# Attention of a hybrid layer on one core: a third k2 buffer in the second half, and another order on VectorE and ScalarE at the end

## The chip, the cores and the metric

The kernel is one program on one core of a Trainium2 chip. The core has a matrix engine (TensorE, PE in the profile; PEld is its loading of weights), a vector engine (VectorE, DVE), a scalar engine (ScalarE, ACT), a general engine (GpSimd, POOL) and a queue engine that mostly issues DMAs (SyncE, SP). Each engine runs its own list of instructions in order and waits on semaphores for the others. All share an on-chip memory, SBUF, of 128 partitions, and the matmuls write to PSUM.

The metric is the device time of one execution in microseconds (us); the median of several executions is given. A trace was taken of one more execution, the profiled one, and everything read from "the profile" or "the trace" belongs to it. L12 is line 12 of the kernel before.

## The reference

The layer has three groups of mixers that read one input projection (an LRU, an attention with forgetting gates, an RWKV-7 recurrence), an output projection, and a gated feed-forward network. The working length is 2064: 16 learned meta tokens, then 2048 tokens. The change lies in the attention (8 heads of 64) and in the start of the output projection:

```python
h += RMSNorm_post( W_out [ RG-LRU group | forgetting-attention group | RWKV-7 group ] ( W_in RMSNorm_pre(h) ) )
h += RMSNorm_post( W_down( gelu(g) * v ) ),  [g | v] = causal_dwconv3( W_up RMSNorm_pre(h) )
```

```python
c = jnp.cumsum(log_f, axis=1)
...
s = einsum('bhqd,bhkd->bhqk', qb, kh) + (cb[..., :, None] - c[..., None, :])
s = jnp.where(kpos[None, :] <= qpos[:, None], s, -jnp.inf)
p = jax.nn.softmax(s, axis=-1)
return einsum('bhqk,bhkd->bhqd', p, vh)
```

Here c is the running sum of the log forget gates of the head. The output must agree with this in float32, so the kernel splits many operands into a rounded high part and the rest (a "split": rounding on ScalarE, subtraction on VectorE) and multiplies the parts.

## The kernel before

**Stages.** The input projection runs first, with the recurrences of the LRU and RWKV groups interleaved. The attention follows; the recurrences' tail runs beside its first part. Then come the output projection in tiles of tokens, the feed-forward network's upper products, and its lower ones. The instructions are written as a Python program; a planner lays them out in lists for the engines. It may move work ahead of what the program says, by its estimate of when inputs are ready. Memory comes from pools. A pool marked `early` may be laid over the space of another that is not yet closed. `tc.issue_after(x)` is an order given by hand: what is made inside the block stands behind instruction x in the list of x's engine (only there).

**The attention.** It goes in two halves: blocks of 512 queries 0 and 1, then 2 and 3; in each half head after head, and for each head its two blocks. A step is one head and one block. For each step there is

- `keys` (once a head): loads three operands. k1 holds the high part and the rest of the keys (L526, L527). k2 holds the keys' high part in its upper 64 rows (L522), a row of ones, and below it two rows of the forget sums, ch and cl (L524, L525). v1 holds the values, whose loads are issued a little later. In the second half a head's keys take a whole buffer; in the first half, half a buffer.
- `maxima`: scores of queries with k2 for the row maximum (L561, with a mask matmul L563 on the diagonal piece), each piece reduced on VectorE (L566); at the end the maximum is turned into a row of the query operand q2 (L571, transposes L574, L575).
- `weights`: the scores (L688 with k1, L689 with k2), the exponential (L693, ACT), the products with the values (L711), and the sum of the weights over the keys in `acc` (L732; one addition in four on VectorE, the others on GpSimd). A group of four key tiles has its values' products one group later.
- `ending`, at the end of a step: the halves of the products are added (L745 on ACT, L748 on DVE). Then three parts are put off by 2, 7 and 12 ticks. `total` splits `acc` (rounding L755 on ACT, subtraction L756 on POOL), sums it over the partitions by two matmuls (L758, L759), copies the sum out (L760) and sends it through memory so that it lies across partitions (L761, L762). `invert` takes reciprocals (L766) and broadcasts them back by two DMAs (L767, L768). `scale` multiplies (L771) and stores the mixed outputs (L772).

`tick` (L797) takes the parts that are due and gives them the order behind `self.reduced`, the latest reduction of a maximum. `run` (L809) interleaves: the maxima are two steps ahead of the weights (`AHEAD = 2`). So after the last maxima two steps of weights are left with no maxima beside them, (7,2) and (7,3) as head and block; the last group of values and the `ending` of (6,3) are written inside (7,2). After them come the parts still put off, and on the last step the DMAs go through GpSimd's queue.

**The buffers.** `Attn.__init__` makes two sets (k1, k2, v1), and `next("k")` (L490) goes round among them; the fixed rows of k2 are written once (`fixed`, L487 and L488, on GpSimd). Since L689 reads k2, a k2 buffer is free again when the scores of its head's second step are done. SBUF pools grow from the left or from the right end. On the right lie `pad`, a tile that only takes up room, and next to it `mt` for the small attention of the meta tokens' own queries, which runs beside the second half (`meta`). Both, and the attention's pool on the left, overlap in space with pools of the input projection and the recurrences, which are closed by then or later. The recurrences' last operations are L1341 (DVE) and L1343 (a store).

**The output tiles.** `w_out_tile` takes 17 tiles of tokens. It loads a tile of the mixed outputs into the one buffer "wr" (L167), splits it into mh (L168, ACT) and ml (L169, DVE), and multiplies it with both parts of the weights: 2 halves of 24 matmuls (L174 to L176). Two tiles' mh and ml fit at once. Tiles 0 to 6 run inside the attention. Tiles 7 and 8 (`HELD = 7, 8`) are ordered behind the values of the last step but one (`at.steps[-2]`). From tile 8 on (`LATE, NORMS = 8, 2`) each tile is followed in the program by the feed-forward norm of up to two tiles: `ffn_norm` scales (L1599, into a buffer that lies over the attention's pool), transposes on PE (L1604) and copies out with `evac` (L57). `evac` goes to ACT and DVE in turn, and when it goes to ACT it stores the instruction in `core.acted`:

```python
self.flip ^= 1
if self.flip:
    self.acted = self.nc.scalar.activation(out, src, AF.Copy)
else:
    self.nc.vector.tensor_copy(out, src)
```

Of the kernel before, what the change touches and what calls it, by code (L numbers as in the profile page):

```python
# [8 lines left out]
F32 = mybir.dt.float32  # L9
F32R = mybir.dt.float32r  # L10
BF16 = mybir.dt.bfloat16
I32 = mybir.dt.int32  # L12
AF = mybir.ActivationFunctionType
ALU = mybir.AluOpType
# [4 lines left out]
P = 128  # L19
D = 1024  # L20
KD = D // P
META = 16
# [423 lines left out]
class Attn:  # L446
# [6 lines left out]

    def __init__(self, core, pool, psum, more, scr):
        self.core, self.pool, self.psum, self.more, self.scr = core, pool, psum, more, scr
        self.wide, self.bank, self.place = False, 0, 0
        nc = self.nc = core.nc
        self.clock, self.later, self.serial, self.added = 0, [], 0, 0
        self.pending, self.loads, self.steps, self.beside = None, [], [], iter(())


        self.turn = {"k": 1, "q2": 0, "q3": 0}
        self.ring = {s: [] for s in self.turn}
        for i in range(self.AHEAD + 1):
            q3 = pool.tile([P, 512], F32R, tag=f"q3_{i}", name=core.n("q3"), bufs=1)
            self.fixed(q3, None, self.ONES)
            self.ring["q3"].append(q3)
            q2 = pool.tile([P, 512], F32R, tag=f"q2_{i}", name=core.n("q2"), bufs=1)
            nc.vector.memset(q2[64:128].bitcast(F32), 0.0)
            self.ring["q2"].append(q2)  # L470
            if i > 1:
                continue
            k1 = pool.tile([P, 2, KHALF], F32R, tag=f"k1_{i}", name=core.n("k1"), bufs=1)
            k2 = pool.tile([P, 2, KHALF], F32R, tag=f"k2_{i}", name=core.n("k2"), bufs=1)
            v1 = pool.tile([P, 2, NKT // 2 + 1, 64], F32, tag=f"v1_{i}", name=core.n("v1"), bufs=1)
            self.fixed(None, k2, self.ONES)
            self.ring["k"].append((k1, k2, v1))

    def fixed(self, q, k, ones):

# [9 lines left out]
    def next(self, s):  # L490
        self.turn[s] = (self.turn[s] + 1) % len(self.ring[s])
        return self.ring[s][self.turn[s]]
# [14 lines left out]
    def keys(self, h, nt):  # L507

        nc, scr = self.nc, self.scr
        n = META + P * (nt - 1)  # L510
        r = slice(64 * h, 64 * h + 64)
        if n <= KHALF:

            i, half = divmod(self.place, 2)
            self.place = (self.place + 1) % 4
            k1, k2, v1 = (t[:, half] for t in self.ring["k"][i])
        else:
            k1, k2, v1 = self.next("k")
            k1, k2 = (t[:].rearrange("p h t -> p (h t)") for t in (k1, k2))
            v1 = v1[:].rearrange("p h j d -> p (h j) d")  # L520
        k1f, k2f = k1.bitcast(F32), k2.bitcast(F32)
        nc.sync.dma_start(k2f[0:64, :n], scr["kh"][r, :n])  # L522
        g = 64 + self.ONES
        nc.sync.dma_start(k2f[g : g + 1, :n], scr["ch"][h : h + 1, :n])  # L524
        nc.sync.dma_start(k2f[g + 1 : g + 2, :n], scr["cl"][h : h + 1, :n])  # L525
        nc.sync.dma_start(k1f[0:64, :n], scr["kh"][r, :n])  # L526
        nc.sync.dma_start(k1f[64:128, :n], scr["kl"][r, :n])  # L527

        def values():
            nc.sync.dma_start(v1[:, : nt - 1], scr["v"][: n - META, r].rearrange("(j p) d -> p j d", p=P))  # L530
            nc.sync.dma_start(v1[:META, nt - 1], scr["v"][n - META : n, r])


        self.loads.append(values)
        return k1, k2, v1
# [120 lines left out]
    def weights(self, h, b, keys, queries, fill):  # L656
# [80 lines left out]
        def ending(po, acc):  # L737


            while len(self.later) > 8:  # L740
                self.later.pop(0)[2]()

            o, oh = self.t([64, 512], "o", bufs=4), self.t([64, 512], "oh")
            c1 = kt[1][2]
            nc.scalar.activation(oh[:, c1:n], po[64:128, c1:n], AF.Copy)  # L745
            if c1:
                nc.scalar.activation(o[:, :c1], po[0:64, :c1], AF.Copy)
            nc.vector.tensor_tensor(o[:, c1:n], po[0:64, c1:n], oh[:, c1:n], op=ALU.add)  # L748
            g = n // 16
            dcol = self.t([16, 32], "dcol", bufs=4)  # L750
            rb, queue = [], self.queue

            def total():
                ah, al = (self.t([P, 512], "oh", F32R) for _ in range(2))
                nc.scalar.activation(ah[:, :n], acc[:, :n], AF.Copy)  # L755
                nc.gpsimd.tensor_tensor(al[:, :n], acc[:, :n], ah[:, :n], op=ALU.subtract)  # L756
                ps = self.mx()
                nc.tensor.matmul(ps[0:1, :n], core.ones_col[:], ah[:, :n], start=True, stop=False)  # L758
                nc.tensor.matmul(ps[0:1, :n], core.ones_col[:], al[:, :n], start=False, stop=True)  # L759
                nc.scalar.activation(acc[0:1, :n], ps[0:1, :n], AF.Copy)  # L760
                queue.dma_start(scr["den"][h : h + 1, ts], acc[0:1, :n])  # L761
                queue.dma_start(dcol[:, :g], scr["den"][h, ts].rearrange("(p c) -> p c", c=g))  # L762

            def invert():
                rb.append(self.t([64, 512], "rb"))
                nc.vector.reciprocal(dcol[:, :g], dcol[:, :g])  # L766
                queue.dma_start(scr["rden"][h, ts].rearrange("(p c) -> p c", c=g), dcol[:, :g])  # L767
                queue.dma_start(rb[0][:, :n], scr["rden"][h : h + 1, ts].broadcast_to([64, n]))  # L768

            def scale():  # L770
                nc.vector.tensor_tensor(o[:, :n], o[:, :n], rb[0][:, :n], op=ALU.mult)  # L771
                queue.dma_start(scr["mix"][256 + 64 * h : 256 + 64 * h + 64, ts], o[:, :n])  # L772

            for d, f in zip(self.DELAYS, (total, invert, scale)):
                self.serial += 1
                self.later.append((self.clock + d, self.serial, f))
            self.later.sort(key=lambda x: x[:2])
# [28 lines left out]

    AHEAD = 2

    def run(self, pool):  # L809


        self.queue = self.nc.sync
        ready = []
        for half, bs in enumerate(((0, 1), (2, 3))):
            if half:
                self.beside = self.meta(pool)
            for h in range(NH):
                self.wide = (half, h) >= WIDE
                keys = self.keys(h, 4 * bs[-1] + 5)
                for b in bs:  # L820
                    gen, total, out = self.maxima(h, b, keys), self.pieces(b), []

                    def fill(share, gen=gen, total=total, out=out):
                        while len(out) < min(total, share * total):
                            out.append(next(gen))

                    if len(ready) == self.AHEAD:
                        self.weights(*ready.pop(0), fill)
                    fill(1.0)
                    ready.append((h, b, keys, next(gen)))  # L830
        for i, step in enumerate(ready):
            if i == len(ready) - 1:
                self.queue = self.nc.gpsimd
            self.weights(*step, lambda share: None)
        self.flush()
        for _ in self.beside:
            pass
        for _, _, f in self.later:
            f()
# [660 lines left out]
    return wh, wl  # L1500


def w_out_tile(core, pool, psum, scr, w, x, meta, gain, s, rows, v):

    nc = core.nc
    wh, wl = w
    mh = pool.tile([P, KD, P], F32R, tag="mh", name=core.n("mh"))
    ml = pool.tile([P, KD, P], F32R, tag="ml", name=core.n("ml"))
    mixed = scr["mix"][:, s : s + rows].rearrange("(k p) t -> p k t", p=P)
    load_parts(core, (pool, "wr", 1), mixed, mh[:, :, :rows], ml[:, :, :rows])  # L1510
    xt = pool.tile([P, D], F32, tag="wx", name=core.n("wx"))
    nc.sync.dma_start(xt[:rows], meta[s : s + rows, :] if s < META else x[s - META : s - META + rows, :])
    halves = []
# [562 lines left out]
def hybrid_block_kernel(ctx: ExitStack, tc: tile.TileContext, args, out):  # L2076
# [8 lines left out]
    def run(gen):  # L2085
        for _ in gen:
            pass

    def pool(es, name, bufs, **kw):
        return es.enter_context(tc.tile_pool(name=name, bufs=bufs, **kw))  # L2090
# [11 lines left out]
    with ExitStack() as p1:  # L2102
# [67 lines left out]
        with ExitStack() as p1b:  # L2170
            more = pool(p1b, "ps_more", 1, space=PSUM, **right, **early)
            at = Attn(core, pool(p1b, "ap", 2, **early), pool(p1b, "ps_at", 1, space=PSUM), more, scr)

            pool(p1b, "pad", 1, **right).tile([P, 24832], F32, name="pad")
            at.run(pool(p1b, "mt", 1, **right, **early))
    qp = pool(ctx, "qp", 1, **early)
    gf = pool(ctx, "gf", 1, **early)
    with ExitStack() as p3:
# [12 lines left out]
        with p2:  # L2191
# [9 lines left out]
            for i, (f, rows) in enumerate(FFN_TILES):  # L2201
                with tc.issue_after(at.steps[-2].ins) if i in HELD else nullcontext():
                    _, rs[i] = w_out_tile(
                        core, wp, banks, scr, w, x, meta, g_post, f + META - HALO, rows, rsv[:, 6 * i : 6 * i + 6]
                    )
                banks.wide = core.root = i >= LATE - 1
                core.apart = not core.root
# [137 lines left out]
```

## Time and profile before

| | |
|---|---|
| runs | 3026.11, 3015.82, 3020.2 us; median 3020.2 us |
| profiled execution | 3012.84 us, of which the span from first to last instruction is 3011.1 us |
| granted TensorE clock, mean over the span | 0.971 |
| core memory traffic | read 368.07 MB, written 158.90 MB |
| attention (with the recurrences' tail) | about 885 to 1551 us |
| output projection after the attention | 1551 us to about 1667 us |
| feed-forward network, upper and lower products | about 1667 to 2560 us, and to the end |

How to read the profile. A row of the timeline has the start in us from the span's begin, the duration in us, the engine, the line, the operation, the output and the inputs by the program's names, the shape, and how many equal instructions in succession it stands for. In brackets stands how long the engine was idle before it and which work ended that idle time. `SPq` is the issuing of a DMA by SyncE's queue. Matmuls overlap, so a row's duration is more than the distance to the next one: while the clock is full, matmuls of 512 columns start every 0.23 us and take 0.39 us each. "Granted clock" is the share of full speed that the throttle let TensorE have. Rows of groups give the count, then the busy time and the mean duration, then the idle time before the group.

### The profile page before, as it was taken

To read this page: it belongs to the slowest core of one execution; us is meant where nothing else is said; L and a number is where in the kernel's file an instruction comes from. 1 tells how busy PE (TensorE), PEld (TensorE's weight loads), DVE (VectorE), ACT (ScalarE), POOL (GpSimd) and SP (SyncE) were. 2 spreads that over 40 slices of the span, in tenths; PEclk is the share of its full clock that TensorE was granted. 3 is DMA by queue.
4 is the path that set the end of the run, shared out by engine and by line. 5 is a ranking of instruction groups with operands and counts; after the bars stand their busy time and mean duration, and the time that the engine had idled before them with its cause. 6 is when DMAs were issued, how large, how long until landed. Compare 5 with 4: busy or idle time off the path is not lost.

```text
span 3011.1 us, 52783 instructions
## 1 busy us (share of the span) xinstructions
PE 2901.2 (96%) x18694; PEld 2487.0 (83%) x18694; DVE 2039.1 (68%) x3937; ACT 1479.4 (49%) x2858; POOL 1314.8 (44%) x1567
## 2 busy tenths in 40 slices
PE   6999999999999999999989999999999999999998
PEld 6998899888886654566558999999999999787887
DVE  5258645665577775555626898798778777656766
ACT  4246333444346654454635666666666665424333
POOL 1002121222124666566843567455644534656443
PEclk8999999999978999999999999999999999999999
DMA  6776569576653347435326565577777764436453
GB/s 212 236 240 217 164 227 310 183 236 218 188 135 81 97 109 212 111 96 124 82 76 230 167 203 177 171 209 211 215 210 218 214 199 131 162 116 220 139 180 119
DMA packets 469190, 530.49 MB, mean 176 GB/s; under 512 B 85710, under 2 KB 355736, under 8 KB 467372
## 3 DMA queue, kind: packets, MB, share of 16 engines
q1 hardware_dynamic: 468156, 526.17, 57.9%
q8 instruction: 147, 2.41, 0.3%
q14 instruction: 119, 0.97, 0.1%
q0 software_dynamic: 768, 0.93, 0.1%
HBM read 368.07 MB, written 158.90 MB: 175 GB/s over the span
## 4 chain that ended last, share of the span: by engine, by line
PE 44%; DVE 2%; DMA 1%; POOL 1%; ACT 1%; issue 1%; SPq 0%; DVEq 0%; POOLq 0%; ACTq 0%
PE psu L174 9%; PE psu L175 9%; PE psu L176 9%; PE psd L174 4%; PE psd L175 4%; PE psd L176 4%; PE pswo L174 1%; PE pswo L176 1%; PE pswo L175 1%; PE pst L1604 1%; DMA uq<-scr_us 0%; POOL dw L1638 0%; DVE uw L1638 0%; PE po L711 0%; POOL u L1903 0%
## 5 line engine op out<-in xcount | busy, mean ns | idle before, releaser
L174 PE MATMUL psu<-xo,uw 128*128 128x344 f32 x1848 | 586.6, 322 | 6.4 <-ACT ga L1809 3.3
L175 PE MATMUL psu<-xo,uw 128*128 128x344 f32 x1848 | 592.2, 321 | 0.0
L176 PE MATMUL psu<-xo,uw 128*128 128x344 f32 x1848 | 581.8, 320 | 0.0
L174 PE MATMUL psp<-xh,wh 128*128 128x384 f32 (+2 forms) x1152 | 380.4, 330 | 0.0
L176 PE MATMUL psp<-xh,wl 128*128 128x384 f32 (+2 forms) x1152 | 377.9, 328 | 0.2 <-DMA wl<-scr_wk 0.2
L175 PE MATMUL psp<-xl,wh 128*128 128x384 f32 (+2 forms) x1152 | 377.2, 327 | 0.0
L1638 DVE TENSOR_TENSOR uw<-uq,uw 128x512 fp32r<-128x512 f32 x341 | 324.9, 957 | 58.0 <-ACT uw L1637 55.2
L174 PEld LDWEIGHTS psu<-xo,uw 128*128 128x128 f32 x1848 | 346.4, 188 | 8.1 <-ACT ga L1809 3.6
L175 PEld LDWEIGHTS psu<-xo,uw 128*128 128x128 f32 x1848 | 347.7, 188 | 0.0
L176 PEld LDWEIGHTS psu<-xo,uw 128*128 128x128 f32 x1848 | 346.2, 188 | 0.0
L1637 ACT ACTIVATE uw<-uq 128x512 fp32r<-128x512 f32 x462 | 288.1, 627 | 94.0 <-PE psu L176 42.9
L693 ACT ACTIVATE p<-sc,bias 128x512 f32<-128x512 f32 (+4 forms) x352 | 197.4, 589 | 187.4 <-PE sc L689 161.4
L566 DVE TENSOR_REDUCE mc<-mx 128x1 f32<-128x512 f32 (+6 forms) x352 | 190.2, 565 | 112.8 <-PE mx L561 85.8
L1777 DVE SCALAR_TENSOR_TENSOR uy<-psu,ffn_cols,uy 128x342 f32<-128x342 f32 (+1 forms) x390 | 220.4, 567 | 59.9 <-ACT uy L1775 57.9
L1785 POOL TENSOR_TENSOR uy<-uy,uy 128x342 f32<-128x342 f32 (+1 forms) x132 | 145.4, 1102 | 240.6 <-DVE uy L1777 59.7
L732 POOL TENSOR_TENSOR acc<-acc,p 128x512 f32<-128x512 f32 (+3 forms) x208 | 221.3, 1067 | 52.1 <-DVE acc L732 24.7
L1638 POOL TENSOR_TENSOR uw<-uq,uw 128x512 fp32r<-128x512 f32 x121 | 177.9, 1470 | 138.8 <-ACT uw L1637 121.1
L174 PEld LDWEIGHTS psp<-xh,wh 128*128 128x128 f32 x1152 | 220.0, 191 | 8.3 <-issue 6.9
L176 PEld LDWEIGHTS psp<-xh,wl 128*128 128x128 f32 x1152 | 219.8, 191 | 7.6 <-issue 5.1
L175 PEld LDWEIGHTS psp<-xl,wh 128*128 128x128 f32 x1152 | 219.9, 191 | 5.0 <-issue 3.2
L1638 DVE TENSOR_TENSOR fo<-u,fo 128x896 fp32r<-128x896 f32 x88 | 101.7, 1155 | 132.0 <-ACT fo L1637 131.5
L1637 ACT ACTIVATE fo<-u 128x896 fp32r<-128x896 f32 x88 | 81.2, 923 | 205.9 <-PE psd L176 117.3
(483 smaller groups left out, 6415.2 us busy)
## 6 DMA issues: line engine op xcount, KB each, us to landing
uq<-scr_us SPq DMA_DIRECT2D x220, 256.0 KB
uq<-in_ffn_up_dram SPq DMA_DIRECT2D x209, 256.0 KB
wl<-scr_wk SPq DMA_DIRECT2D x48, 512.0 KB
wh<-scr_wk SPq DMA_DIRECT2D x48, 512.0 KB
u<-scr_ff SPq DMA_DIRECT2D x88, 256.0 KB
scr_ff<-uy SPq DMA_DIRECT2D x110, 171.0 KB
raw<-in_w_in_dram SPq DMA_DIRECT2D x24, 512.0 KB
scr_wk<-wh SPq DMA_DIRECT2D x24, 512.0 KB
```

What stands on the lines that cost most here:

```text
L174: nc.tensor.matmul(out, ah, bh, start=first, stop=False, skip_group_check=more)
L175: nc.tensor.matmul(out, ah, bl, start=False, stop=False, skip_group_check=more)
L176: nc.tensor.matmul(out, al, bh, start=False, stop=last, skip_group_check=more)
L566: self.reduced = nc.vector.tensor_reduce(mc[:rows, i, ci : ci + 1], ps[:rows, : e - a], axis=AX.X, op=ALU.max)
L693: last = nc.scalar.activation(p[:rows, :w], ps[:rows, :w], AF.Exp, bias=bias[:rows, j : j + 1])
L732: eng.tensor_tensor(a, ps_[0][0][:rows, c0:n] if start and i == 1 else a, p[:rows, : n - c0], op=ALU.add)
L1604: nc.tensor.transpose(ps[:, k, :rows], xt[:rows, k0 : k0 + P], core.ident[:rows, :rows])
L1637: core.nc.scalar.activation(hi, src, AF.Copy)
L1638: (eng or core.nc.vector).tensor_tensor(lo, src, hi, op=ALU.subtract)
L1777: core.conved = stt(y[:, :n], src[:, i : n + i], cw[:, 44 * i + cc : 44 * i + cc + 1], y[:, :n], op0=ALU.mult, op1=ALU.add)
L1785: core.pooled = nc.gpsimd.tensor_tensor(v[:, :n], g[:, :n], v[:, :n], op=ALU.mult)
```

## The change

1. k2 gets a ring of its own, `k2`, apart from the ring of (k1, v1). At the start of the second half a third k2 is made in a new right-hand pool below `mt`, with its fixed rows; `pad` is cut by 960 floats a partition (3840 B; a k2 buffer has 8320 B). The first turn in the second half goes to the new buffer (head 0), then buffers 0, 1, new, and so on.
2. Before the last two steps of weights `tail` is set. From then on `reduced` is the latest addition of products (L748), so the parts that are due stand behind it on DVE.
3. `total` stores its rounding (L755) in `core.acted`.
4. `w_out_tile` takes a list of instructions behind which its load and split are ordered. Tile 9 (`HELD[-1] + 1`) gets `core.acted` and `at.reduced`, as they are when tile 9 is written.

```diff
-        self.turn = {"k": 1, "q2": 0, "q3": 0}
+        self.turn = {"k": 1, "k2": 1, "q2": 0, "q3": 0}
...
-            k2 = pool.tile([P, 2, KHALF], F32R, tag=f"k2_{i}", name=core.n("k2"), bufs=1)
+            self.rear(pool, f"k2_{i}")
...
-            self.fixed(None, k2, self.ONES)
-            self.ring["k"].append((k1, k2, v1))
+            self.ring["k"].append((k1, v1))
+
+    def rear(self, pool, tag):
+        k2 = pool.tile([P, 2, KHALF], F32R, tag=tag, name=self.core.n("k2"), bufs=1)
+        self.fixed(None, k2, self.ONES)
+        self.ring["k2"].append(k2)
...
-            k1, k2, v1 = (t[:, half] for t in self.ring["k"][i])
+            k1, v1 = (t[:, half] for t in self.ring["k"][i])
+            k2 = self.ring["k2"][i][:, half]
         else:
-            k1, k2, v1 = self.next("k")
+            (k1, v1), k2 = self.next("k"), self.next("k2")
...
-            nc.vector.tensor_tensor(o[:, c1:n], po[0:64, c1:n], oh[:, c1:n], op=ALU.add)
+            summed = nc.vector.tensor_tensor(o[:, c1:n], po[0:64, c1:n], oh[:, c1:n], op=ALU.add)
+            if self.tail:
+                self.reduced = summed
...
-                nc.scalar.activation(ah[:, :n], acc[:, :n], AF.Copy)
+                core.acted = nc.scalar.activation(ah[:, :n], acc[:, :n], AF.Copy)
...
             if half:
+                self.rear(third, "k2_2")
                 self.beside = self.meta(pool)
...
+        self.tail = True
         for i, step in enumerate(ready):
...
-    load_parts(core, (pool, "wr", 1), mixed, mh[:, :, :rows], ml[:, :, :rows])
+    with ExitStack() as order:
+        for ins in after:
+            order.enter_context(core.tc.issue_after(ins.ins))
+        load_parts(core, (pool, "wr", 1), mixed, mh[:, :, :rows], ml[:, :, :rows])
...
-            pool(p1b, "pad", 1, **right).tile([P, 24832], F32, name="pad")
-            at.run(pool(p1b, "mt", 1, **right, **early))
+            pool(p1b, "pad", 1, **right).tile([P, 23872], F32, name="pad")
+            at.run(pool(p1b, "mt", 1, **right, **early), pool(p1b, "k2", 1, **right, **early))
...
+                        (core.acted, at.reduced) if i == HELD[-1] + 1 else (),
```

More of the change, by code (lines that the diff above doesn't have):

```diff
@@ L455, in __init__ @@
         self.core, self.pool, self.psum, self.more, self.scr = core, pool, psum, more, scr
-        self.wide, self.bank, self.place = False, 0, 0
+        self.wide, self.bank, self.place, self.tail = False, 0, 0, False
         nc = self.nc = core.nc
@@ L807, with run @@
     AHEAD = 2
-    def run(self, pool):
+    def run(self, pool, third):
         self.queue = self.nc.sync
@@ L1500, in w_out_load, with w_out_tile @@
     return wh, wl
-def w_out_tile(core, pool, psum, scr, w, x, meta, gain, s, rows, v):
+def w_out_tile(core, pool, psum, scr, w, x, meta, gain, s, rows, v, after=()):
     nc = core.nc
@@ L2203, in hybrid_block_kernel @@
                     _, rs[i] = w_out_tile(
-                        core, wp, banks, scr, w, x, meta, g_post, f + META - HALO, rows, rsv[:, 6 * i : 6 * i + 6]
+                        core, wp, banks, scr, w, x, meta, g_post, f + META - HALO, rows, rsv[:, 6 * i : 6 * i + 6],
+                        (core.acted, at.reduced) if i == HELD[-1] + 1 else (),
                     )
```

## The prediction

> **What bounds the kernel now.** I read the head of the page first, then the busy time of each engine by stage, then the waits of TensorE in the attention, and last the timeline around each place that the diff touches.
>
> ```profile
> span 3011.1 us, 52783 instructions
> ...
> PE 2901.2 (96%) x18694; PEld 2487.0 (83%) x18694; DVE 2039.1 (68%) x3937; ACT 1479.4 (49%) x2858; POOL 1314.8 (44%) x1567
> ```
>
> TensorE (PE) is busy 96% of the span, so the time moves only where PE idles, or runs slower after idling. The change takes no matmul away. By stage (columns: stretch, its length, busy time of PE, its weight loads, DVE, ACT, POOL, then granted clock, DMA share, GB/s):
>
> ```profile
> 1080.00:1106.00 26.00, 25.91 (x219) 16.65 (x215) 18.06 (x49) 14.98 (x34) 16.93 (x26) 1.00 0.72 155
> 1106.00:1126.00 20.00, 16.11 (x79) 10.04 (x78) 17.79 (x43) 10.12 (x21) 12.84 (x24) 0.91 0.30 73
> 1126.00:1140.00 14.00, 10.09 (x36) 3.86 (x35) 7.71 (x18) 3.43 (x7) 3.50 (x3) 0.82 0.76 142
> ...
> 1125.00:1551.00 426.00, 398.80 (x1792) 231.94 (x1791) 236.80 (x478) 210.21 (x381) 286.44 (x371) 0.98 0.45 115
> ```
>
> From 1125 to 1551, roughly the attention's second half, PE idles 426.0 - 398.8 = 27.2 us; the change can win a part of that. The stretch 1106 to 1140 already has a thin cover: PE idles 3.9 of 20 us and 3.9 of 14, at a lower clock.
>
> **The keys.** A step's maxima (L561), and later the second matmul of its scores (L689), read k2, the keys with their two rows ch and cl (L522, L524, L525). Two buffers go round among the heads, so a head's keys load only when the head two before has done its scores. PE waited for them three times in the second half:
>
> ```profile
> 1315.37 0.66 PE L561 MATMUL mx<-k,q 128*128 128x400 f32 x2 [1.05 <-DMA k<-scr_cl]
> 1424.86 1.01 PE L561 MATMUL mx<-k,q 128*128 128x400 f32 x3 [2.17 <-DMA k<-scr_cl]
> 1467.51 0.80 PE L561 MATMUL mx<-k,q 128*128 128x400 f32 x3 [1.63 <-DMA k<-scr_cl]
> ...
> 1309.32 0.28 SPq L525 DMA_DIRECT2D k<-scr_cl  x1
> ...
> 1462.50 0.24 SPq L525 DMA_DIRECT2D k<-scr_cl  x1
> ...
> L561 PE MATMUL mx<-k,q 128*128 128x512 f32 (+6 forms) x352 | 131.2, 415 | 16.9 <-DVE mc L566 6.5 <-DMA k<-scr_cl 4.8 <-ACT q L575 2.9
> ...
> L566 DVE TENSOR_REDUCE mc<-mx 128x1 f32<-128x512 f32 (+6 forms) x352 | 190.2, 565 | 112.8 <-PE mx L561 85.8
> ```
>
> These are 1.05 + 2.17 + 1.63 = 4.85 us. The last load was issued 6.0 and 5.0 us before the matmul; a third buffer lets it go about one head earlier, so the wait vanishes unless the DVE reduction that frees the maxima's bank (L566, 565 ns a piece) is late next; over the whole kernel it holds PE longer than the keys do, 6.5 us against 4.8 (the row of L561: busy time, mean ns, then the idle time before it and what ended it). Bounds 0 and -5.5 (with some slow clock after the 2.17); I take -4.5, since a reduction ends well within the gaps. The longer SP queue costs nothing here: five key DMAs a head as before, only earlier.
>
> **The first use of the third buffer.** The diff sets the turn so that head 0 of the second half takes the new buffer, the only one not used before. It is laid below the pool of the meta queries, over space that the recurrences hold. What that means is seen in the neighbour pool, which is laid over the same space:
>
> ```profile
> 1125.52 0.22 DVE L1341 TENSOR_TENSOR rwxu<-rwxu,rps 128x64 f32<-128x64 f32 x1
> 1125.53 0.21 POOL L487 MEMSET mt<- 64x128 f32 x1
> ...
> 1086.16 0.43 SPq L525 DMA_DIRECT2D k<-scr_cl  x1
> ...
> 1106.89 0.39 PE L561 MATMUL mx<-k,q 128*128 128x512 f32 x1
> ...
> 876.29 3.60 POOL L487 MEMSET k<- 64x2080 f32 x2
> ```
>
> The first write into that space comes 0.01 us after the start of the recurrences' last DVE operation. Head 0's keys were loaded at 1086 and used from 1106.89. In the new place they cannot start before about 1125.5: a 64x2080 fill (3.60 for two, so 1.8) and the 1x2080 fill of the same length, about 1.8, then the rows' load of 5 to 6, make 1125.5 + 3.6 + 5 = 1134. What else PE has (the last weights of the first half) covers until about 1121, as its own gaps in 1106 to 1126 close when the 13 maxima pieces leave. From 1134 these pieces run at the reduction's pace, 13 x 0.565 = 7.3, so the step's scores start near 1134 + 7.3 + 2 = 1143 (an estimate). Before:
>
> ```profile
> 1139.74 0.80 PE L688 MATMUL sc<-q,k 128*128 128x512 f32 x1
> ```
>
> That is 3.3 late; some six pieces of the following step, done by then before, are still owed, about 6 x 0.42 = 2.5; and a gap of over 10 us slows the clock, some 2. Sum +8. Bounds: -2, if the recurrences, with DVE less loaded (17.79 of 20 us), end much earlier; +16, if the whole hole of 1121 to 1134 is lost, with 3 of slow clock. I take the middle, +8. POOL's fills stand ahead of its accumulations (L732), which is in the same bounds.
>
> **The scalings behind the sums.** During the last two weights steps, scalings (L771) wait on DVE for a broadcast, and the head's own sum is queued behind:
>
> ```profile
> 1504.09 0.94 DVE L771 TENSOR_TENSOR o<-o,rb 64x512 f32<-64x512 f32 x1 [4.89 <-DMA rb<-scr_rden]
> 1504.95 1.23 DVE L732 TENSOR_TENSOR acc<-acc,p 16x16 f32<-16x16 f32 x1
> ...
> 1506.21 0.63 ACT L755 ACTIVATE oh<-acc 128x512 fp32r<-128x512 f32 x1 [2.11 <-DVE acc L732]
> 1506.89 0.40 PE L758 MATMUL mx<-oh,ones_col 128*1 128x512 f32 x1 [2.28 <-ACT oh L755]
> 1507.61 0.79 PE L688 MATMUL sc<-q,k 128*128 128x512 f32 x1 [0.31 <-ACT p L693]
> ...
> 1508.62 0.63 PE L688 MATMUL sc<-q,k 128*128 128x512 f32 x1
> ...
> 1509.61 2.38 PE L711 MATMUL po<-p,v 128*64 128x512 f32 x8
> ```
>
> DVE idles 4.89 us for the broadcast, so the 16x16 addition, L755 and L758 come late, and PE stands 2.28 us. With sum and addition first, L755 starts near 1504.5 and L758 near 1505.1: -1.8. After the gap matmuls take 0.63 where others take 0.39 to 0.40 (rows below), about five of them and one group of values: -1.5. I take -3.3; bounds -1.5 and -4. The scaling itself lands about a microsecond later behind its sum, and with it one store of mixed outputs.
>
> The Trainium skill ("TensorE: Matmul & The Clock Gate", Part 1: The HAM clock gate) says that PE falls to half clock after an idle window of about 3.4 us. By that rule the 2.28 would cost no clock and the gain 1.5 smaller; the trace shows slow matmuls right behind it, and decides.
>
> **The end of the attention.** Here the last total's rounding is to run ahead of output tile 9's split:
>
> ```profile
> 1543.36 3.65 PE L711 MATMUL po<-p,v 128*64 128x512 f32 x18
> ...
> 1548.00 1.06 ACT L168 ACTIVATE mh<-raw 128x1024 fp32r<-128x1024 f32 x1 [4.20 <-DMA raw<-scr_mix]
> ...
> 1549.09 1.22 DVE L169 TENSOR_TENSOR ml<-raw,mh 128x1024 fp32r<-128x1024 f32 x1 [4.02 <-ACT mh L168]
> 1551.02 0.63 ACT L755 ACTIVATE oh<-acc 128x512 fp32r<-128x512 f32 x1 [1.34 <-DVE acc L732]
> 1551.70 0.58 PE L758 MATMUL mx<-oh,ones_col 128*1 128x512 f32 x1 [4.69 <-ACT oh L755]
> 1552.95 0.79 PE L174 MATMUL pswo<-woh,mh 128*128 128x512 f32 x1 [0.67 <-DVE wx L1542]
> ...
> 1560.09 0.59 ACT L760 ACTIVATE acc<-mx 1x512 f32<-1x512 f32 x1 [5.35 <-PE mx L759]
> ...
> 1574.62 0.68 DVE L771 TENSOR_TENSOR o<-o,rb 64x512 f32<-64x512 f32 x1 [4.93 <-DMA rb<-scr_rden]
> ...
> 1579.13 1.28 DVE L1599 SCALAR_TENSOR_TENSOR xt<-xt,rsv,g_fpre 128x1024 f32<-128x1024 f32 x1
> ...
> 1586.36 1.03 PE L1604 MATMUL pst<-ident,xt 128*128 128x128 f32 x8
> 1587.35 0.58 ACT L57 ACTIVATE q<-pst 128x512 f32<-128x512 f32 x1
> ```
>
> Counting from 1547.0, where L711 ends: PE idles 4.69 + 0.67, and output matmuls start at +5.95, with a half of tile 9. With rounding and split (1.06 + 1.22) out of the way L758 comes at about +2.85, and tile 8, whose split is long done, starts behind L760 at +4.6: a gain of 1.3. But the diff hands tile 9 `core.acted` as it stands when tile 9 is traced. Between the last total and that point the code traces the FFN norms of its first two tiles (LATE and NORMS, L2016), and their evacuation (L57) sets `core.acted` anew. So tile 9's rounding is queued behind an evacuation, not behind L755. That one is reached through L760, the DMA round trip, L771 (1575.30 - 1560.09 = 15.2 us by these rows), two L1599 (the first on 2x1024, about as long; their space is the attention's, so they wait for L771), transposes and L57: 4.6 + 15.2 + 2.6 + 1.0 + 0.6 = +24, then the rounding to +25, and tile 9's matmuls from +25.5. Tile 8 has 48 matmuls, spaced 0.23:
>
> ```profile
> 1561.74 0.40 PE L176 MATMUL pswo<-woh,ml 128*128 128x512 f32 x1
> 1561.97 0.39 PE L174 MATMUL pswo<-woh,mh 128*128 128x512 f32 x1
> ```
>
> It ends at 4.6 + 48 x 0.23 + 2.5 (slow start) = +18. PE then idles about 8 us and starts slow again, 2; tile 10 cannot step in, as its raw buffer (one of them) is free only after tile 9's split. Tile 9 is done at 25.5 + 11 + 2 = +38.5; before, the 96 matmuls of both tiles, from 1552.95 on, ended with the slow start at 1552.95 + 22 + 2.5, which is +30.5. So +8; I take +7.5, for the 1.3 may come out larger. Bounds -3, if the rounding is behind L755 after all, and +10.
>
> **Sum.** -4.5 + 8 - 3.3 + 7.5 = +7.7 on the profiled execution, 3012.84 us (span 3011.1 and 1.7 around it), so 3020.5. The median of the runs shown, 3020.2, is 1.0024 times that execution; on it the forecast is 3028.
>
> **Rivals.**
> *All as intended.* The planner starts the new buffer as early as the old one (head 0 at 0) and the rounding stands behind L755. Then -4.85, -3.3, and at the end -1.3 with up to 2.5 of slow clock saved: -12, 3000.8, on the median 3008. For it: three waits on the keys stand plainly in the trace. Against it: the mt fill at 1125.53, and L57 standing between.
> *Both new waits dear.* Head 0's keys as one mechanism decide: PE finds no cover between 1121 and 1134 (+16), and the evacuation is at its +10: -4.5 - 3.3 + 16 + 10 = 18.2, so 3031, on the median 3038. It is dearer than the forecast once the keys land after 1136. For it: PE clock is down to 0.82 in that stretch already. Against: L1341 may end earlier.
> *The change does not do what it says.* The keys come earlier but the matmuls then wait for DVE's reduction, which the row of L561 already names as its longest wait, so -1; the planner finds cover for head 0 (+3), and the end comes out even: -1 - 3.3 + 3 = -1, on the median 3019.
>
> **How the numbers follow.** What a measurement of this kernel can tell from no change is about 0.3%, 9 us. Forecast 0.40, its own range 3019 to 3037 (the bounds of head 0 and of the end, not both at an extreme), so 0.22 within 0.3%, 0.17 slower, 0.01 faster. As intended 0.22: 0.19 faster, 0.03 same. Both dear 0.28: all slower. Not as it says 0.10: 0.08 same, 0.01 to each side. Faster 0.21, same 0.33, slower 0.46. The range reaches to the other cases' times, 3008 and, with the head-0 price a little past its bound, 3040.
>
> **What would show it.** Keys: no row of L561 with an idle for `k<-scr_cl` after 1160; waits for L566 in their place show the third rival. Head 0: the k fills on POOL and the first L561 of the second half, at 1107 or at 1134, and the PE busy time of 1106 to 1160. Scalings: L758 near 1505 with a gap under 1 us. End: whether tile 9's L168 stands behind L755 or behind L57, and whether PE idles some 8 us between tile 8 and tile 9. It is wrong if head 0's keys are loaded before the recurrences end, or if PE never waits for tile 9.

## The result and the profile after

The changed kernel took 3011.41 us (median of 19 runs, 3000.95 to 3020.22), the kernel before 3017.54 us (median of 19 runs, 3012.41 to 3026.11). The ratio is 0.9978, with a 95% interval of 0.9968 to 0.9987. So it is 0.22% faster, where 0.3% slower had been forecast. The time lies within the whole range given (3008 to 3040 us), but below the forecast's own part of it (3019 to 3037), and the sign is wrong.

Here is the head of the page of the changed kernel. Its profiled execution (3015.7 us) is the second longest of its 19 runs:

```profile
span 3014.0 us, 52809 instructions
...
PE 2901.1 (96%) x18694; PEld 2488.9 (83%) x18694; DVE 2037.7 (68%) x3937; ACT 1480.0 (49%) x2858; POOL 1324.4 (44%) x1569
```

This span is 2.9 us longer than that of before, though the median is 6 us shorter. So the two traces cannot be laid on each other from the start; they need landmarks. A good one is the first operation of a step's `ending`, the copy L745 on ACT, which is L750 in the changed kernel (its lines from 490 on stand some 4 to 12 further down: L561 is L566, L571 is L576, L755 is L762, L758 is L765, L760 is L767, L771 is L778, L1599 is L1611, L1604 is L1616). Here are five landmarks in the timeline of before: the ends of steps (0,5,0), (1,0,3), (1,6,3) and (1,7,3), as half, head and block, and the first product of the feed-forward network.

```profile
1076.83 0.50 ACT L745 ACTIVATE oh<-po 64x400 f32<-64x400 f32 x1
...
1193.35 0.59 ACT L745 ACTIVATE oh<-po 64x512 f32<-64x512 f32 x1
...
1503.51 0.59 ACT L745 ACTIVATE oh<-po 64x512 f32<-64x512 f32 x1 [0.50 <-PE po L711]
...
1549.08 0.59 ACT L745 ACTIVATE oh<-po 64x512 f32<-64x512 f32 x1
...
1660.19 0.32 PE L174 MATMUL psu<-xo,uw 128*128 128x344 f32 x1
```

The same in the changed kernel:

```profile
1082.91 0.50 ACT L750 ACTIVATE oh<-po 64x400 f32<-64x400 f32 x1
...
1196.40 0.59 ACT L750 ACTIVATE oh<-po 64x512 f32<-64x512 f32 x1 [0.93 <-PE po L716]
...
1497.00 0.60 ACT L750 ACTIVATE oh<-po 64x512 f32<-64x512 f32 x1 [0.51 <-PE po L716]
...
1536.94 0.59 ACT L750 ACTIVATE oh<-po 64x512 f32<-64x512 f32 x1 [3.06 <-PE po L716]
...
1662.36 0.32 PE L174 MATMUL psu<-xo,uw 128*128 128x344 f32 x1
```

The first landmark is already 6.1 us later. Up to there both traces hold equally many instructions on TensorE (8593), VectorE (1768), ScalarE (921) and GpSimd (411), so these 6.1 us are spread between executions. The differences of neighbouring landmarks are what the change can answer for (us, the second less the first of each pair):

| stretch | before | after | after - before | forecast |
|---|---|---|---|---|
| A: (0,5,0) to (1,0,3), first use of the new buffer | 116.5 | 113.5 | -3.0 | +8 |
| B: (1,0,3) to (1,6,3), the keys of heads 1 to 7 | 310.2 | 300.6 | -9.6 | -4.5 |
| C: (1,6,3) to (1,7,3), the last sums and scalings | 45.6 | 39.9 | -5.6 | -3.3 |
| D: (1,7,3) to the first upper product | 111.1 | 125.4 | +14.3 | +7.5 (with the end of C) |

The rest, to the end of the span, is 1350.9 and 1351.6. The sum from (0,5,0) on is -3.2 in these two executions. Three stretches gained more than forecast, and one lost more. The border between C and D moves by itself, though. Before, the copy L745 stands behind tile 9's split on ACT and starts 2.1 us after the last values (1549.08 - 1547.01); in the changed kernel it comes first, at once after them (1536.94 - 1536.90). So some 2 us of C's gain and of D's loss are only this, and C and D together are +8.7 us (165.4 against 156.7).

**Stretch B** shows in the groups of TensorE's lines from 1170 to 1530 us, which is B and some 25 to 30 us on either side of it (count, busy time, mean ns, then idle time before the group and what ended it). Before:

```profile
L688 PE MATMUL sc<-q,k 128*128 128x512 f32 (+4 forms) x209 | 83.2, 399 | 3.6 <-ACT p L693 3.3
L561 PE MATMUL mx<-k,q 128*128 128x512 f32 (+4 forms) x199 | 69.0, 395 | 8.5 <-DMA k<-scr_cl 4.8 <-DVE mc L566 1.9 <-DVE sh L571 1.6
L758 PE MATMUL mx<-oh,ones_col 128*1 128x512 f32 x15 | 6.0, 399 | 4.1 <-ACT oh L755 2.3 <-DVE mc L566 1.8
```

After:

```profile
L693 PE MATMUL sc<-q,k 128*128 128x512 f32 (+4 forms) x220 | 85.8, 391 | 2.8 <-ACT p L698 2.5
L566 PE MATMUL mx<-k,q 128*128 128x512 f32 (+4 forms) x203 | 71.5, 394 | 1.7 <-DVE mc L571 1.6
L765 PE MATMUL mx<-oh,ones_col 128*1 128x512 f32 x15 | 5.9, 395 | 0.2
```

The 4.8 us for the keys are gone, and nothing took their place. The maxima's idle time fell from 8.5 to 1.7 us: the waits named for VectorE's row of maxima (L571 before) went as well. Those in front of the sums (L758) went too, but 1.57 of their 1.8 us stand at 1178.17, in A. In B alone (1193.35 to 1503.51 us, and 1196.40 to 1497.00) TensorE idled 11.4 us before and 2.2 after, so 9.2 of the 9.6 us gained are idle time, and 4.8 of them had been named as waits for the keys.

**Stretch A** in the timeline of the changed kernel:

```profile
1123.82 0.22 DVE L1350 TENSOR_TENSOR rwxu<-rwxu,rps 128x64 f32<-128x64 f32 x1
...
1126.53 1.83 POOL L491 MEMSET k<- 64x2080 f32 x1
...
1128.69 0.25 SPq L530 DMA_DIRECT2D k<-scr_cl  x1
...
1131.29 1.82 POOL L492 MEMSET k<- 1x2080 f32 x1
...
1133.16 1.07 PE L566 MATMUL mx<-k,q 128*128 128x400 f32 x3 [0.59 <-POOL k L492]
```

The new buffer does wait for the recurrences, as forecast. The last thing that the maxima waited for was not the load of the keys but the second fill (L492), which started 2.9 us after the first had ended, with other work of GpSimd between the two. And L1350, the recurrences' last VectorE operation (L1341 before), now comes 40.9 us after the first landmark (1123.82 - 1082.91), against 48.7 before (1125.52 - 1076.83). The reductions of head 0's maxima are no longer between the recurrences' operations on VectorE; before, all 13 stood there, from 1110.23 us on.

**Stretch D**, the end, in the timeline of the changed kernel:

```profile
1539.63 0.56 PE L765 MATMUL mx<-oh,ones_col 128*1 128x512 f32 x1 [2.73 <-ACT oh L762]
...
1541.61 0.59 ACT L767 ACTIVATE acc<-mx 1x512 f32<-1x512 f32 x1 [2.03 <-PE mx L766]
...
1546.75 3.90 SPq L1725 DMA_DIRECT2D uq<-in_ffn_up_dram  x4
...
1560.02 0.68 DVE L778 TENSOR_TENSOR o<-o,rb 64x512 f32<-64x512 f32 x1 [8.89 <-DMA rb<-scr_rden]
...
1561.32 1.42 DVE L1553 SCALAR_TENSOR_TENSOR pswo<-pswo,rs,g_post 128x512 f32<-128x512 f32 x2
1562.65 1.27 DVE L1611 SCALAR_TENSOR_TENSOR xt<-xt,rsv,g_fpre 2x1024 f32<-2x1024 f32 x1
...
1563.97 1.01 PE L1616 MATMUL pst<-ident,xt 2*128 2x2 f32 x8 [9.08 <-DVE xt L1611]
...
1566.45 3.15 PE L1616 MATMUL pst<-ident,xt 128*128 128x128 f32 x12 [1.47 <-DVE xt L1611]
...
1567.58 0.60 ACT L57 ACTIVATE q<-pst 128x512 f32<-128x512 f32 x1 [1.07 <-PE pst L1616]
1568.07 1.05 ACT L168 ACTIVATE mh<-raw 128x1024 fp32r<-128x1024 f32 x1
```

Tile 9's rounding L168 stands right behind L57, and TensorE idles 9.08 + 1.47 us between tiles 8 and 9. This is the forecast's mechanism. Its size is not: the round trip from L767 to the end of L778 took 1560.70 - 1541.61 = 19.1 us in place of 15.2. A store of 2 KB in it landed late. DMA issues of before, 1560 to 1577 us (KB, median us from issue to landing):

```profile
scr_rden<-dcol POOLq DMA_DIRECT2D x1, 2.0 KB, 1.6
```

and of the changed kernel, 1541 to 1562 us, where four loads of the upper weights (256 KB each) were issued in that time:

```profile
scr_rden<-dcol POOLq DMA_DIRECT2D x1, 2.0 KB, 5.4
```

### The profile page after: what moved, and what is told of

Its sections match the earlier page's. It is cut to its first block, busy times and chain, and to the rows that moved or that the text cites. A ratio compares the mean times of both kernels' runs of the same rounds, so it can differ in the third digit from the quotient of the medians.

```text
span 3014.0 us, 52809 instructions
## 1 busy us (share of the span) xinstructions
PE 2901.1 (96%) x18694; PEld 2488.9 (83%) x18694; DVE 2037.7 (68%) x3937; ACT 1480.0 (49%) x2858; POOL 1324.4 (44%) x1569
## 4 chain that ended last, share of the span: by engine, by line
PE 59%; DVE 5%; POOL 2%; issue 2%; ACT 2%; DMA 1%; SPq 0%; DVEq 0%; POOLq 0%; ACTq 0%
PE psu L174 9%; PE psu L175 9%; PE psu L176 9%; PE po L716 4%; PE psd L174 4%; PE psd L175 4%; PE psd L176 4%; PE mx L566 2%; PE sc L693 2%; PE pswo L174 2%; PE pswo L176 2%; PE pswo L175 2%; PE sc L694 2%; DVE mc L571 1%; ACT p L698 0%
## 5 line engine op out<-in xcount | busy, mean ns | idle before, releaser
L571 DVE TENSOR_REDUCE mc<-mx 128x1 f32<-128x512 f32 (+6 forms) x352 | 190.2, 565 | 117.8 <-PE mx L566 84.3
```

The source lines that it names most:

```text
L571: self.reduced = nc.vector.tensor_reduce(mc[:rows, i, ci : ci + 1], ps[:rows, : e - a], axis=AX.X, op=ALU.max)
```

## The experiments

All ratios are to the kernel before, run beside on the same chip. Stretches are read from the same five landmarks as above.

| kernel | median us (before) | ratio, 95% interval | A | B | C | D |
|---|---|---|---|---|---|---|
| changed | 3011.4 (3017.5) | 0.9978, 0.9968 to 0.9987 | 113.5 | 300.6 | 39.9 | 125.4 |
| e1 buffer alone | 2999.7 (3021.1) | 0.9930, 0.9911 to 0.9949 | 115.6 | 300.7 | 43.1 | 110.5 |
| e2 tail alone | 3013.4 (3021.1) | 0.9974, 0.9959 to 0.9989 | 114.7 | 312.2 | 42.8 | 111.4 |
| e3 without tile 9's order | 3001.3 (3021.1) | 0.9925, 0.9906 to 0.9944 | 113.6 | 301.4 | 41.9 | 110.0 |
| e4 tile 9 behind the total | 3004.1 (3021.1) | 0.9935, 0.9916 to 0.9953 | 113.8 | 303.0 | 39.9 | 111.5 |
| e5 old buffer first | 3001.6 (3017.1) | 0.9945, 0.9926 to 0.9963 | 116.7 | 301.9 | 42.0 | 110.0 |
| e6 new buffer once | 3006.2 (3017.1) | 0.9961, 0.9948 to 0.9975 | 111.9 | 310.6 | 42.4 | 111.0 |
| e7 both mended | 3000.2 (3017.1) | 0.9944, 0.9924 to 0.9964 | 114.5 | 304.4 | 39.9 | 111.4 |
| e8 tile 9's order alone | 3026.4 (3019.8) | 1.0028, 1.0014 to 1.0042 | 117.4 | 315.0 | 43.8 | 125.3 |
| e9 loads later | 3006.2 (3019.8) | 0.9962, 0.9948 to 0.9977 | 113.8 | 300.7 | 39.9 | 121.5 |

**e1: the third buffer alone.** Parts 2 and 4 are taken out of the changed kernel:

```diff
-        self.tail = True
...
-                        (core.acted, at.reduced) if i == HELD[-1] + 1 else (),
```

> Part 1 of the change alone (the third k2 buffer), the scalings and tile 9 in the order of before. Theory: in the trace of the changed kernel TensorE idles 11.8 us less between 1170 and 1536 us, and only 4.85 of the 16.6 before were named as waits for the keys, so the buffer alone brings most of it: 9 to 13 us below the kernel before, and no end cost. Rival (the prediction's sizes): 4.5 gained on the keys, 8 lost on head 0, so 2 to 5 us above.

It is 21 us faster by the medians, at least 15 by the interval, which is more than the theory said and the opposite of the rival. The trace holds about 14 of it (A -1.0, B -9.5, C -2.5, D -0.6); the rest is within the spread of single executions.

**e2: the tail alone.** The kernel before with `summed`, `tail` and `reduced` of the diff.

> Part 2 of the change alone (parts that are due queued behind the last sums). Theory: the gap of 2.28 us at L758 near 1507 and the slow matmuls behind it go, 2 to 4 us below the kernel before. Rival: the gap is filled but the scaling's delay returns at the end, within 1 us of before.

0.26% faster, between 3 and 12 us. In the trace the stretch that it touches, C, is 2.8 us shorter, and the gap at the first sum near the end of (1,6,3) is 0.62 in place of 2.28:

```profile
PE mx L760 <- ACT oh L757: 0.6, 1, 0.6
```

(TensorE's waits of e2, 1170 to 1530 us: total, times, longest.) So the mechanism of the theory holds, and its 2 to 4 us fit the trace; the medians differ by 7.7 us, more than that, but the interval reaches down to 3. Its B is the same work as before in the same order, and took 2.0 us more: such is the spread of one execution.

**e3: the change without part 4**, and **e4: tile 9 behind the last total's own rounding.**

```diff
-                        (core.acted, at.reduced) if i == HELD[-1] + 1 else (),
```

```diff
-                core.acted = nc.scalar.activation(ah[:, :n], acc[:, :n], AF.Copy)
+                core.acted = self.rounded = nc.scalar.activation(ah[:, :n], acc[:, :n], AF.Copy)
...
-                        (core.acted, at.reduced) if i == HELD[-1] + 1 else (),
+                        (at.rounded, at.reduced) if i == HELD[-1] + 1 else (),
```

> The changed kernel without part 4 (tile 9 ordered as before). Theory: the order behind the evacuation costs 11 us of idle TensorE between the tiles against about 1.5 won at L758, so without it the time is 8 to 12 us below the changed kernel, near 3001. Rival: the idle is taken from slack later (the wait for ACT ga before the upper products), and the time stays within 3 us of the changed kernel.

> The changed kernel, with tile 9's split behind the last total's own rounding (kept under a name of its own) in place of core.acted as it stands then. Theory: L57 is what holds the split back; so here it follows the rounding of the last total at once, no 9 us gap at the transposes, and the time is 10 to 14 us below the changed kernel, 1 to 3 below the kernel without part 4. Rival (the wait of L1599 for the last scaling holds TensorE whatever tile 9 does): the gap stays, within 3 us of the changed kernel.

e3 is 10 us below the changed kernel by the medians, e4 7 us; by the ratios, which take out what the chips differ in, it is 16 and 13. Both drop the 14 us of stretch D, so L57 held tile 9 back, not the wait for the last scaling as such. The second half of e4's expectation failed: it isn't below e3. The timeline of e4 shows the order that the diff describes,

```profile
1542.11 0.63 ACT L762 ACTIVATE oh<-acc 128x512 fp32r<-128x512 f32 x1 [1.47 <-DVE acc L737]
1542.65 1.04 ACT L168 ACTIVATE mh<-raw 128x1024 fp32r<-128x1024 f32 x1
...
1544.77 0.59 ACT L767 ACTIVATE acc<-mx 1x512 f32<-1x512 f32 x1 [1.08 <-PE mx L766]
```

but C and D together are 151.4 us in e4 and 152.0 in e3. The output matmuls do start earlier, 4.5 us behind the last values (1544.54 - 1540.01) against 5.9 in e3 (1545.92 - 1540.00), though they stand behind the second matmul of the total (L766). That is the gain of 1.3 that the prediction named for the case that the rounding is behind L755. Of it 1.0 us is lost again at a transpose (L1616 at 1579.01, for a copy on VectorE). The rest of the 2 us between the two kernels' C is the moved border.

**e5: head 0 on an old buffer**, no order for tile 9.

```diff
-        self.turn = {"k": 1, "k2": 1, "q2": 0, "q3": 0}
+        self.turn = {"k": 1, "k2": 2, "q2": 0, "q3": 0}
```

> Parts 1 and 2 without part 4, and the ring of k2 turned so that head 0 takes an old buffer and head 2 is the first on the new one, whose space is free by then. Theory (head 0's late keys cost nothing, since VectorE bounds that stretch and the following step makes it up): within 3 us of the same kernel with the new buffer first, near 3001. Rival (the prediction's price of head 0): 6 to 10 us below it, near 2993.

3001.6 us by the median, as the theory said. By the ratios it is 6 us slower than e3, with overlapping intervals; it is not 6 to 10 us faster, so the prediction's price of head 0 is refuted. In the trace head 0 on the new buffer is even the better one, 113.6 against 116.7 here in A. Over all kernels the two cases overlap a little, though: 111.9 to 115.6 with head 0 on the new buffer (changed, e1, e3, e4, e6, e9), 114.5 to 117.4 with it on an old one (before, e2, e5, e7, e8). What does not overlap is the end of the recurrences. It is late again here, 1126.06 - 1078.42 (the first landmark of e5) = 47.6 us behind it:

```profile
1126.06 0.22 DVE L1350 TENSOR_TENSOR rwxu<-rwxu,rps 128x64 f32<-128x64 f32 x1
```

It is 47.6 to 50.0 us in the five kernels with head 0 on an old buffer, and 40.8 to 41.1 in the six with it on the new one.

**e6: the new buffer for head 0 alone**, on e3.

```diff
                 keys = self.keys(h, 4 * bs[-1] + 5)
+                if half and h == 0:
+                    self.ring["k2"].pop()
+                    self.turn["k2"] = 1
```

> As e3, but the new buffer serves head 0 alone; then the two old ones alternate, so heads 1 and 2 still load early and heads 3 to 7 wait for the head two before, as in the kernel before. Theory (the gain comes from maxima that no longer stand still before each head: 7 to 8 us each at heads 4 to 7 before, 4.85 us of it shown as idle for keys): 5 to 8 us of the gain are lost, near 3008, and the three idle times for k<-scr_cl are back. Rival (the gain is in the first two heads, where the loads moved most): within 3 us of e3.

5 us above e3 by the medians (11 by the ratios), B 9.2 us longer, and the waits for the keys are back, five in place of the three expected (TensorE's waits, 1170 to 1530 us):

```profile
PE mx L566 <- DMA k<-scr_cl: 7.4, 5, 1.9
```

TensorE's idle time in B is 11.4 us again, as before the change. So the gain comes head by head, and the theory holds against the first-two-heads rival.

**e7: both faults mended** (the edits of e4 and e5 together).

> The whole change with both suspected faults mended: head 0 on an old buffer and tile 9 behind the last total's own rounding. Theory: no better than e3 and e5 by more than 3 us, since the start of the output tiles is then held by the wait for L766 instead; 2998 to 3004. Rival (as intended): each mend is worth what the prediction put on it, 2990 to 2994.

3000.2 us: the mends add nothing to e3 and e5 that these runs can tell. The third buffer is what pays: with it and without L57 ahead of tile 9 all of e1, e3, e4, e5 and e7 are 0.55 to 0.75% faster than before, more than the 0.4% of the rival "all as intended".

**e8: part 4 alone** (with part 3), on the kernel before.

> Part 4 (with part 3) alone on the kernel before: tile 9's rounding behind core.acted as it stands then. Theory: the chain from the last total to L57 does not depend on the other parts, so TensorE idles 7 to 11 us between tiles 8 and 9 and the time is 8 to 13 us above the kernel before. Rival (the cost exists only because the earlier end of the attention runs ahead of other loads): within 4 us of before.

0.28% slower, 4 to 13 us. The trace has the full cost, C and D 169.1 us against 156.7, and the same gap:

```profile
1586.70 1.01 PE L1607 MATMUL pst<-ident,xt 2*128 2x2 f32 x8 [9.85 <-DVE xt L1602]
...
1590.31 0.60 ACT L57 ACTIVATE q<-pst 128x512 f32<-128x512 f32 x1 [1.07 <-PE pst L1607]
1590.80 1.05 ACT L168 ACTIVATE mh<-raw 128x1024 fp32r<-128x1024 f32 x1
```

The medians differ by 6.6 us, and the ratio makes it 8.5, at the low end of the 8 to 13 expected. The rival's 4 us lie just outside the interval, and the gap is there without an earlier end of the attention.

**e9: the four weight loads behind tile 10's**, in the whole change. `core.ten` is `core.loaded` as it stands after tile 10, and the first four loads behind it go through

```diff
-        self.core.nc.sync.dma_start(raw[:], src)
+        core = self.core
+        core.uq = getattr(core, "uq", 0) + 1
+        with core.tc.issue_after(core.ten.ins) if hasattr(core, "ten") and core.uq <= UQ0 + 4 else nullcontext():
+            core.nc.sync.dma_start(raw[:], src)
```

> The whole change, and the first four loads of the upper weights (256 KB each) issued behind the load of output tile 10, so that none lies beside the last total's round trip. Theory (contention: the store of the reciprocals landed after 5.4 us beside these loads and after 1.6 us without them): from L767 to the end of L778 about 15 us in place of 19.1, the gap at the transposes 3 to 5 us shorter, 3 to 5 us below the changed kernel. Rival (the round trip is as long anyway): 19 us, within 2 us of the changed kernel.

```profile
1538.49 0.59 ACT L767 ACTIVATE acc<-mx 1x512 f32<-1x512 f32 x1 [2.03 <-PE mx L766]
...
1552.94 0.68 DVE L778 TENSOR_TENSOR o<-o,rb 64x512 f32<-64x512 f32 x1 [5.57 <-DMA rb<-scr_rden]
...
1556.89 1.01 PE L1616 MATMUL pst<-ident,xt 2*128 2x2 f32 x8 [6.49 <-DVE xt L1611]
```

The round trip is 1553.62 - 1538.49 = 15.1 us, the gap 2.6 us shorter (under the 3 to 5 expected), D 3.9 us shorter, and the median 5 us below that of the changed kernel. The intervals of the two ratios overlap, so the run times alone do not settle it. The traces do: e8 has the same four loads beside its round trip and takes 19.0 us, with the store landing after 5.5. So these loads made the difference between 15 and 19 us. They are not the only ones that count, for e4 took 17.3 us with one of them issued beside it and e7 18.1 with none; which of the other loads does it there was not tested.

## Why the prediction was wrong

**The first use of the third buffer (+8, measured -3) is the step that failed and that turned the sign.** The forecast took the recurrences' end, 1125.5, from the old trace and counted everything from there. But that end was itself set by what was to be moved: 13 reductions of 0.565 us, 7.3 us in all, on VectorE, which had 17.8 of 20 us busy in that stretch. Without them the recurrences end 7.8 us earlier, head 0's maxima start 50.3 us behind the first landmark (1133.16 - 1082.91) in place of the 57 forecast, and the 13 pieces run off in 7.5 us, with one short operation of others between them. The prediction named this as its bound of -2, and took the middle all the same (+8; the middle of -2 and +16 is 7). The price of +8 is refuted by e5, and the earlier end of the recurrences stands in every kernel with head 0 on the new buffer. That it comes from VectorE's share and not from TensorE's is read from the timeline; no run separates the two. Nor is the sign of the -3 certain, since A overlaps between the two cases. The time from the recurrences' last operation to the maxima came out near the forecast (1133.16 - 1123.82 = 9.3 us for 8.6) with some luck: the forecast put a load last, and a late second fill was.

**The keys (-4.5, measured -9.6) were sized by the waits named for them.** The mechanism was right, and e6 confirms it: fewer buffers, waits back. But 4.85 us was only the part of the delay that carries the keys' name; in B 9.2 us of idle time went. The kernels with the old ring, or most of it (before, e2, e6, e8), have 310 to 315 us in B with 11.4 to 13.2 of idle time; those with three buffers throughout have 301 to 304, with 2.2 to 5.7. Under which name the rest of the idle time stands differs: L571's 1.6 of before is missing in e6, which has 7.4 for the keys, and waits for the reductions of the maxima are 0.8 us in B with the change but 3.6 in e5. That late keys crowd the maxima and so cause the other waits is thus a guess; the runs show only that idle time goes with the third buffer.

**The scalings (-3.3)** were sized well: e2's C is 2.8 us shorter. On top of the third buffer little of it is left (e3 against e1: C 1.2 us shorter, the medians equal within the intervals), since the gap at the sum is 1.19 us there already.

**The end (+7.5, measured 12.4 to 13.4)** went as told: L758 came 2.7 us behind the last values in place of 4.7, tile 8 ran from 4.5 to 18.0 us behind them (forecast 4.6 and 18), tile 9's rounding stood behind L57, and TensorE idled between tiles 8 and 9. e3, e4 and e8 show each part of it. By C and D together, part 4 costs 12.4 us in e8 alone (169.1 - 156.7) and 13.4 in the changed kernel against e3 (165.4 - 152.0). Missing in the sum were 4 us of contention (e9) and 1.4 us of tile 8's own scaling (L1553) on VectorE between L778 and L1611. The prediction took the round trip from a stretch in which the DMA engines moved 112 GB/s on average (1560.09 to 1575.30); in the changed kernel it was 200 (1541.61 to 1560.70). The Trainium skill ("DMA: Bandwidth & Descriptors", Latency and other measured facts) gives 0.2 us for an access to device memory on average and 2 us at high load. That is one access and not a whole store, but the direction agrees: the same 2 KB store took 1.6 us before, 2.0 in e9, and 5.4 beside the loads.

**Rivals and clock.** "All as intended" came nearest in time, but by luck: its gain at the end did not come, and its price of the keys was too small. "Both dear" fell with head 0's price, and "The change does not do what it says" with the row of the changed kernel's L566, 1.6 us for the reductions. The gap of 2.28 us is gone with the change, but e8 keeps the order of before there and has it again:

```profile
1519.37 0.39 PE L758 MATMUL mx<-oh,ones_col 128*1 128x512 f32 x1 [2.27 <-ACT oh L755]
...
1520.79 0.66 PE L688 MATMUL sc<-q,k 128*128 128x512 f32 x1
```

Matmuls of 0.66 us follow 2.27 us of idle, as before. So here the row was the better guide than the rule that the prediction takes from the Trainium skill ("TensorE: Matmul & The Clock Gate", Part 1: The HAM clock gate), idle windows of about 3.4 us. But the length of a single gap does not decide it either. In e2 a longer gap is followed by matmuls at full speed (granted clock 1.00 from 1432 to 1440 us):

```profile
1432.12 0.77 PE L561 MATMUL mx<-k,q 128*128 128x400 f32 x3 [2.37 <-DMA k<-scr_cl]
...
1433.08 0.40 PE L689 MATMUL sc<-q,k 128*128 128x512 f32 x1
```

and in e6 a shorter one by slow ones (granted clock 0.50 from 1300 to 1302 us):

```profile
1297.92 0.80 PE L566 MATMUL mx<-k,q 128*128 128x400 f32 x3 [1.41 <-DMA k<-scr_cl]
...
1299.24 0.63 PE L174 MATMUL pswo<-woh,mh 128*128 128x512 f32 x1
```

What decides it is left open by these runs.

**The forecast as a whole** added four terms. Head 0 and the keys were too high by 11 and 5 us, the end was too low by 5 to 6, so that part of the errors cancelled and the number came nearer than its terms. Measured, the terms are -3.0 (A), -9.6 (B), -4.7 in C and D together without part 4 (e3; 3.0 of it already in e1, with the buffer alone) and +13.4 for part 4, which makes -3.9; the runs say -4 to -10.

## What to carry to other kernels

A resource that is late because of work X has to be timed without X's load when the change moves that very load: here the recurrences ended 8 us earlier once the maxima waited for them. The time named for a wait need not be its whole price: 4.8 us were named for the keys here, and 9.2 us of idle time went with the third buffer. And an order given against a shared variable, as `core.acted`, means whatever wrote it last: look up every writer between the place where it is meant and the place where it is read; leaving the order out, or naming the right instruction, was worth 7 to 16 us.

## What the runs showed of the hardware

Executions of the same instruction list were up to 11 us apart by the end of step (0,5,0) (1074.1 us in e6, 1085.2 in e3), more than the whole effect of 6 us. Only differences between landmarks, and medians of interleaved runs, told the parts apart.
